# Where the last block's high parts are kept, and the order of the queue, at the start of the second SwiGLU product

## The chip, the cores and the metric

The kernel runs on one core of one Trainium2 chip. The metric is the device time of one execution in microseconds (us); the time of a kernel is the median of its runs. The engines are called as in the profile: PE (TensorE, matrix products), DVE (VectorE), ACT (ScalarE), POOL (GpSimd) and SP (SyncE, which here issues nearly all DMA transfers).

## The reference

One step of a decoder trunk with two layers, for a prompt of 1024 positions and 8 samples of 4 positions that share the weights. Layer 0 mixes tokens with windowed attention, layer 1 with a recurrent block. After each mixer comes a SwiGLU, and this is the part that the change concerns:

```python
def swiglu(h, w_in, w_out):
    g, u = jnp.split(h @ w_in, 2, axis=-1)
    return (jax.nn.silu(g) * u) @ w_out

# in every layer
xp = xp + yp
xs = xs + ys
xp = xp + swiglu(rms_norm(xp, ffn_norm[layer]), w_ffn_in[layer], w_ffn_out[layer])
xs = xs + swiglu(rms_norm(xs, ffn_norm[layer]), w_ffn_in[layer], w_ffn_out[layer])
```

The model width is 1024, the inner width 2816 (22 blocks of 128), all in 32-bit floats. One more output of layer 0 matters here: the new caches of the samples, most of which is a plain copy of the old ones.

## The kernel before, in words

**Tiles.** Columns are positions: 1056 of them in three column tiles, t = 0 and 1 of 384 and t = 2 of 288 (the end of the prompt and the samples). A product in 32-bit precision is made of three matrix products of rounded parts: `mm3` takes the high and the low part of the weights and of the data. A high part is a rounded copy made by ACT, the low part is the difference, made by DVE.

**First product.** `ffn_phase` goes through the 22 inner blocks. The first two are done plainly (`ins`); the other twenty by `blocks(f)`: `seven` treats t = 0 and 1 together as a 2 x 2 block scheme with seven products in place of eight, and `h_in` treats t = 2. The result of a block does not stay on the core: `keep` makes the high and the low part and stores both to `od` in device memory. Its source for the high part is one buffer of tag `hi` or, every second time, one of two buffers of tag `xs`. A pair of blocks gives seven such results for t = 0 and 1: the even block stores one of them, `keep_pair` of the odd block the other six. `h_in` stores one of its own.

**Second product.** `second` builds 20 units, five chunks of four blocks, with four units `mp` to a chunk. A unit gives two of the eight row blocks of the output. It has 66 matrix products: six for each of seven block products, and two times twelve of `plain` for t = 2. Its operands are the nine tiles of its chunk, in the order b11, t3, b21, t2, two for t = 2, t4, t1, b22, which `fetch(c, i, j)` loads from `od`. `add` adds each partial result onto the residual stream x on DVE (line 1026); these adds keep the order in which they are written. PE then goes on to accumulate in the same bank, so it waits for the add. The residual stream was put aside in device memory (`xd`) and comes back by `reload(0)` (row blocks 0 to 3, used by a chunk's units 0 and 1) and `reload(1)` (row blocks 4 to 7, used by units 2 and 3).

**Weights of a unit.** `Mixed` has three steps: `load` (line 151, DMA into one of two buffers `raw`), `parts` (`fill`: ACT at line 136 and DVE at line 137; then four sums on POOL, lines 157 to 160, that turn `raw` into the mixed weights), and `sums` (`fill` again on the mixed weights). Unit u's first step inside, `s0`, comes behind its third block product: it fetches three operands of the next chunk, does the `sums` of unit u + 1 and the `load` of unit u + 3. Behind the fourth product come the `parts` of unit u + 2. From `pin(True)` on, these keep their place among the adds on DVE.

**Order.** PE and SP issue in the order in which the program is written. ACT, DVE and POOL are put in order by a scheduler when the program is built, and then work through their lists in that order. `lead` is the hand-written order of the transition: the steps between and behind the last two blocks (`y` and `z`). `lead[3]` is the `mid` of the last block's `seven`, that is, behind its matrix products and ahead of its `keep_pair`; `lead[4]` comes behind that, ahead of the last `h_in`. In the kernel before, `lead[3]` queues six operands and `reload(1)`; the twelve stores of `keep_pair` follow; unit 2's weights come behind them.

**Places.** Large tiles live in 18 slots, taken from the front of a list and given back at its end (`act_tile`, `freeall`). In layer 0, `caches(b)` queues two copies from device memory to device memory ahead of each of the units 0 to 7.

Of the kernel before, what the change touches and what calls it, by code (L numbers as in the profile page):

```python
# [6 lines left out]
F32 = mybir.dt.float32  # L7
# [5 lines left out]
P = 128  # L13
# [9 lines left out]
DB, DS = 8, 4  # L23
# [12 lines left out]
WMAX = 384  # L36
# [129 lines left out]
class Whole:  # L166
# [5 lines left out]
    load = Mixed.load  # L172
# [81 lines left out]
class Kern:  # L254
# [589 lines left out]
    def ffn_phase(self, l, before, after):  # L844
# [7 lines left out]
        T, HD_, OD = {}, {}, {}  # L852
# [36 lines left out]
        def keep(dst, src):  # L889
            W = src.shape[-1]  # L890
            T["n"] = T.get("n", 0) + 1
            hi = self.tmp([P, WMAX], "hi", bufs=1) if T["n"] % 2 else \
                self.gt.tile([P, WMAX], F32, name=self.nm("hi"), tag="xs", bufs=2)
            hi = hi[:, :W]
            nc.scalar.activation(hi.bitcast(F32R), src, AF.Copy)  # L895
            tt(src.bitcast(F32R), src, hi, OP.subtract)
            nc.sync.dma_start(dst[:, 0, :], hi)
            nc.sync.dma_start(dst[:, 1, :], src)

        def keep_pair(f, h0, h1):  # L900

            c, j, half = place(f)
            g = lambda tag: self.gt.tile([P, WMAX], F32, name=self.nm("t"), tag=tag, bufs=2)
            od = lambda i: OD[c, i][:, j]
            if half == 0:
                st1 = T["even"] = (g("acc"), h1)
                tt(st1[0], h1, h0, OP.subtract)
                keep(od("b11"), h0)
                return
            t1, b12 = T.pop("even")  # L910
            t2, t4 = g("rs"), g("acc")
            tt(t2, h1, t1, OP.subtract)
            tt(b12, h1, b12, OP.subtract)
            tt(t4, h0, t2, OP.subtract)
            for i, x in zip(KEEP[1:], (h0, h1, t1, t2, b12, t4)):
                keep(od(i), x)


        def h_in(wg, wu, f, t, mid=(), last=False):
            W = WID[t]  # L920
            g = self.proj(wg, self.xn[t], W)
            for fn in mid:
                fn()
            u = self.proj(wu, self.xn[t], W)
            if last:
                self.freeall(self.xn[t])

            def post():
                sg = self.tmp([P, WMAX], "sg")
                nc.scalar.activation(sg[:, :W], g[:, :W], AF.Silu)  # L930
                tt(sg[:, :W], u[:, :W], sg[:, :W], OP.mult)
                c, j, half = place(f)
                keep((OD[c, j] if f >= NPL else HD_[t])[:, half], sg[:, :W])

            return post
# [32 lines left out]
        def unring():  # L968
            self.ring = []
            self.freeall(T["ring"])  # L970

        def reload(i):
            for t in range(NT):
                if i == 0:
                    self.xt[t] = []
                self.xt[t].append(self.act_tile([P, 4, WMAX], F32, "x"))
                nc.sync.dma_start(self.xt[t][i][0][:, :, :WID[t]], self.xd[t][:, 4 * i:4 * i + 4, :])
# [50 lines left out]
        def h_out(w0, w1, h, t, steps):  # L1028
            W = WID[t]
            ws = (w0, w1)  # L1030
            for m in range(KB):
                ps = self.bank()
                for c in range(2):
                    self.mm3(ps[:, :W], ws[c][:, 0, m * P:(m + 1) * P], ws[c][:, 1, m * P:(m + 1) * P],
                             h[:, c, 0, :W], h[:, c, 1, :W], c == 0, c == 1)
                x = self.xview(t, m)
                with tc.high_priority(PRI):
                    tt(x, ps[:, :W], x, OP.add)  # L1038
                if l == 1 or t < 2:
                    with tc.high_priority(PRI if t == 2 else 0):  # L1040
                        self.square(t, m, SQUARES[l][t][m])
                for fn in steps.get(m, ()):
                    fn()
# [12 lines left out]
        def unit(w, ws, o, mp, steps):  # L1056


            b11, t3, b21, t2, h0, h1, t4, t1, b22 = o
            m0, m1 = 2 * mp, 2 * mp + 1  # L1060

            def prod(ps, w, q, x, first):
                for j in range(2):
                    c = slice(q * 256 + j * P, q * 256 + (j + 1) * P)
                    self.mm3(ps[:, :WMAX], w[:, 0, c], w[:, 1, c], x[:, j, 0, :], x[:, j, 1, :],
                             first and j == 0, j == 1, not first)

            A, B, Dk = self.bank(), self.bank(), self.bank()
            prod(A, w, 0, b11, True)
            add(0, m0, A)  # L1070
            prod(Dk, ws, 2, t3, True)
            add(1, m1, Dk)
            prod(B, w, 1, b21, True)
            add(0, m0, B)
            steps[0]()
            prod(A, ws, 0, t2, False)
            add(0, m1, A)
            steps[1]()
            plain(w, (h0, h1), m0)
            prod(Dk, w, 3, t4, False)  # L1080
            add(0, m1, Dk)
            prod(A, ws, 3, t1, False)
            add(1, m1, A)
            plain(w, (h0, h1), m1)
            prod(A, ws, 1, b22, False)
            add(1, m0, A)
# [4 lines left out]
        def ins(f, mid=((), (), ())):  # L1091
            w = pair(f)
            return [Item(lambda a, b, t=t: h_in(a, b, f, t, mid[t]), w, w if t == 2 else []) for t in range(NT)]
# [7 lines left out]
        def second():  # L1101

            O = [[Operand(lambda c=c, i=i: OD[c, i], WMAX if isinstance(i, str) else WID[2], pools)
                  for i in ("b11", "t3", "b21", "t2", 0, 1, "t4", "t1", "b22")] for c in range(NCH)]
            M = [Mixed(I[f"wz{l}"][c, mp]) for c in range(NCH) for mp in range(4)]
            n = len(M)
            M += [Whole(I[f"wd{l}"][k]) for k in range(2)]
            H = [Operand(lambda t=t: HD_[t], WID[t], pools) for t in range(NT)]
            gate = Gate()

            def do(u, what):
                if u < len(M):
                    getattr(M[u], what)(self)

            def fetch(c, i, j):
                for o in O[c][i:j]:
                    assert o.prep(self)

            def pin(on):
                self.pinned = on  # L1120

            lead = [[lambda: reload(0), lambda: fetch(0, 0, 3)], [lambda: do(0, "load")],
                    [lambda: do(0, "parts"), lambda: do(0, "sums"), lambda: do(1, "load")],
                    [lambda: fetch(0, 3, 9), lambda: reload(1)], [lambda: do(1, "parts"), lambda: do(2, "load")],
                    [lambda: pin(True)], [lambda: pin(False), ring]]
            items = []
            for u in range(n):
                c, mp = divmod(u, 4)

                def s0(u=u, c=c, mp=mp):  # L1130
                    if mp < 3 and c + 1 < NCH:
                        fetch(c + 1, 3 * mp, 3 * mp + 3)
                    if mp < 3 and c + 1 == NCH:
                        assert H[mp].prep(self)
                    do(u + 1, "sums")
                    do(u + 3, "load")
                    gate.open = u == n - 1

                st = (s0, lambda u=u: do(u + 2, "parts"))
                p = [M[u].w, M[u].s]  # L1140
                items.append(Item(lambda a, b, *y, mp=mp, st=st: unit(a, b, y, mp, st), p + O[c],
                                  p + (O[c] if mp == 3 else []), [gate]))
            w = [x.w for x in M[n:]]
            steps = [{}, {2: n0[1:2], 5: n0[3:4]}, {2: n1[1:2], 5: n1[3:4]} if l else {3: n1[1:2], 6: n1[3:4]}]
            last = [Item(lambda a, b, h, t=t: h_out(a, b, h, t, steps[t]), w + [H[t]],
                         (w if t == 2 else []) + [H[t]], [gate]) for t in range(NT)]
            return lead, items, last

        L = [enter]
        a = ins(0, (before[1], (), ()))  # L1150
        b = ins(1, (before[3], (), ()))
        s = [lambda j=j: sums(j) for j in range(4)]
        L += before[0] + [a[0]] + before[2] + [b[0]] + before[4] + s[:2] + [a[1]] + s[2:] + [b[1]]
        L += [lambda: self.freeall(self.xn[1][:2]), a[2], b[2]]
        lead, units, p = second()
        for f in range(NPL, NF - 2):
            L += blocks(f)
# [1 line left out]
        z[0].mid = lead[3]  # L1159
        L += lead[0] + [y[0]] + lead[1] + [y[1]] + lead[2] + [z[0]] + lead[4] + [z[1]] + lead[5]  # L1160
        for i, x in enumerate(units):
            if l == 0 and i < DB:
                L.append(lambda b=i: self.caches(b))
            L.append(x)
        L += lead[6] + p[:2] + n0[4:] + [p[2]] + n1[4:]
        if l == 0:
# [377 lines left out]
```

## Time and profile before

| | us |
|---|---|
| median of 3 runs | 2177.17 |
| lowest and highest | 2175.77, 2177.6 |
| the profiled execution's own time | 2174.34 |
| its span in the profile | 2171.3 |
| PE busy in the span | 2117.0 |
| PE's mean granted clock | 0.991 |

The profiled execution is 2.8 us under the median, and its time lies 3.0 us above its span. Times in the views are microseconds from the start of the span. The second product of layer 0 begins at about 847.7, that of layer 1 at about 1907.7. In a time line each row is a start, a duration, an engine, a line of the kernel, an operation, output and inputs by the program's names, and a count; brackets give the idle time of the engine before it and what ended it. Names: `o` operands, `od` the stored results, `x` the residual stream, `xd` the stream put aside, `raw` weights as loaded, `w` their parts, `mm` a bank of results.

### The profile page before, as it was taken

To read this page: it belongs to the slowest core of one execution; us is meant where nothing else is said; L and a number is where in the kernel's file an instruction comes from. 1 tells how busy PE (TensorE), PEld (TensorE's weight loads), DVE (VectorE), ACT (ScalarE), POOL (GpSimd) and SP (SyncE) were. 2 spreads that over 40 slices of the span, in tenths; PEclk is the share of its full clock that TensorE was granted. 3 is DMA by queue.
4 is the path that set the end of the run, shared out by engine and by line. 5 is a ranking of instruction groups with operands and counts; after the bars stand their busy time and mean duration, and the time that the engine had idled before them with its cause. 6 is when DMAs were issued, how large, how long until landed. Compare 5 with 4: busy or idle time off the path is not lost.

```text
span 2171.3 us, 35218 instructions
## 1 busy us (share of the span) xinstructions
PE 2117.0 (97%) x13608; PEld 2093.8 (96%) x13608; DVE 1480.6 (68%) x2889; ACT 1005.4 (46%) x1835; POOL 253.4 (12%) x342
## 2 busy tenths in 40 slices
PE   9999999999999998999999989999999999989997
PEld 9899989999999998999999989999999999989997
DVE  6877787756656665666686787787666656556666
ACT  5666665434444343121268887754444444421112
POOL 1223231000000001322200000000000000022223
PEclk9999999999999999999999999999999999999999
DMA  5332335233343248755211123442343343585532
GB/s 194 100 102 85 116 125 179 100 105 130 116 154 133 101 153 328 283 215 187 94 49 59 59 82 113 148 154 78 126 144 133 105 158 120 219 318 216 209 141 80
DMA packets 131631, 310.10 MB, mean 143 GB/s; under 512 B 14152, under 2 KB 84872, under 8 KB 131464
## 3 DMA queue, kind: packets, MB, share of 16 engines
q1 hardware_dynamic: 130128, 306.95, 40.8%
q8 instruction: 106, 1.74, 0.3%
q10 hardware_dynamic: 1336, 0.92, 0.1%
q14 instruction: 61, 0.50, 0.1%
HBM read 223.15 MB, written 86.65 MB: 143 GB/s over the span
## 4 chain that ended last, share of the span: by engine, by line
PE 85%; DVE 6%; ACT 4%; DMA 3%; issue 1%; POOL 1%; SPq 0%; DVEq 0%; ACTq 0%; POOLq 0%
PE mm L314 81%; DMA o<-od 1%; ACT w L85 1%; DVE w L89 1%; PE pt L635 1%; PE s L587 1%; DVE s L605 1%; ACT s L612 1%; DMA od<-hi 1%; DMA raw<-in_wz 0%; DVE xn L353 0%; ACT g L1262 0%; PE mm L383 0%; DVE g L1310 0%; DVE pr L353 0%
## 5 line engine op out<-in xcount | busy, mean ns | idle before, releaser
L314 PE MATMUL mm<-xn,w 128*128 128x384 f32 (+1 forms) x5808 | 928.7, 318 | 12.3 <-DVE w L89 5.2
L314 PEld LDWEIGHTS mm<-xn,w 128*128 128x128 f32 x5808 | 903.2, 188 | 18.0 <-DVE w L89 6.3
L314 PE MATMUL mm<-o,w 128*128 128x384 f32 (+1 forms) x2928 | 474.0, 323 | 19.7 <-DVE x L1026 19.7
L314 PEld LDWEIGHTS mm<-o,w 128*128 128x128 f32 x2928 | 470.6, 189 | 20.8 <-DVE x L1026 20.8
L314 PE MATMUL mm<-T,w 128*128 128x384 f32 x1920 | 347.1, 336 | 0.1
L314 PEld LDWEIGHTS mm<-T,w 128*128 128x128 f32 x1920 | 334.8, 188 | 0.5 <-ACT e L999 0.4
L89 DVE TENSOR_TENSOR w<-raw,w 128x1024 fp32r<-128x1024 f32 x202 | 245.8, 1224 | 115.1 <-ACT w L85 113.6
L1026 DVE TENSOR_TENSOR x<-mm,x 128x384 f32<-128x384 f32 x360 | 191.2, 534 | 139.9 <-PE mm L314 139.0
L85 ACT ACTIVATE w<-raw 128x1024 fp32r<-128x1024 f32 x204 | 214.9, 1056 | 126.8 <-PE mm L314 65.9
L136 ACT ACTIVATE w<-raw 128x1024 fp32r<-128x1024 f32 x84 | 85.3, 1053 | 327.2 <-POOL raw L160 295.5
L157 POOL TENSOR_TENSOR raw<-raw 128x256 f32<-128x256 f32 x40 | 29.5, 738 | 1188.2 <-DVE w L137 1188.2
L137 DVE TENSOR_TENSOR w<-raw,w 128x1024 fp32r<-128x1024 f32 x84 | 102.8, 1224 | 15.4 <-ACT w L136 15.4
L627 POOL TENSOR_SCALAR s<-s,sm 128x256 f32<-128x256 f32 (+1 forms) x128 | 84.5, 679 | 203.9 <-DVE sm L625 84.3
L314 PE MATMUL mm<-att,w 128*128 128x384 f32 (+1 forms) x576 | 97.3, 325 | 0.0
L314 PEld LDWEIGHTS mm<-att,w 128*128 128x128 f32 x576 | 91.4, 188 | 1.9
L314 PE MATMUL mm<-y,w 128*128 128x384 f32 (+1 forms) x576 | 93.1, 322 | 0.0
L314 PEld LDWEIGHTS mm<-y,w 128*128 128x128 f32 x576 | 91.9, 188 | 0.0
L895 ACT ACTIVATE hi<-e 128x384 fp32r<-128x384 f32 x80 | 41.8, 523 | 87.4 <-DVE e L1017 33.1
L612 ACT ACTIVATE s<-s,sm 128x256 f32<-128x256 f32 (+1 forms) x128 | 61.7, 483 | 41.9 <-DVE sm L609 41.8
L118 DVE TENSOR_TENSOR w<-raw,w 128x1024 fp32r<-128x1024 f32 x40 | 48.9, 1222 | 35.9 <-ACT w L116 35.8
L374 ACT ACTIVATE sq<-x 128x384 f32<-128x384 f32 (+1 forms) x105 | 51.0, 492 | 38.2 <-DVE x L1038 18.0
L1001 DVE TENSOR_TENSOR sg<-mm,sg 128x384 f32<-128x384 f32 x40 | 22.2, 555 | 61.4 <-PE mm L314 61.4
(204 smaller groups left out, 2266.1 us busy)
## 6 DMA issues: line engine op xcount, KB each, us to landing
o<-od SPq DMA_DIRECT2D x70, 768.0 KB, 6.8
od<-hi SPq DMA_DIRECT2D x140, 192.0 KB, 2.0
raw<-in_wg SPq DMA_DIRECT2D x44, 512.0 KB, 4.1
raw<-in_wu SPq DMA_DIRECT2D x44, 512.0 KB, 4.5
raw<-in_wz SPq DMA_DIRECT2D x40, 512.0 KB, 3.7
od<-e SPq DMA_DIRECT2D x80, 192.0 KB, 2.0
raw<-in_wq SPq DMA_DIRECT2D x24, 512.0 KB, 3.6
raw<-in_wo SPq DMA_DIRECT2D x24, 512.0 KB, 3.6
```

What stands on the lines that cost most here:

```text
L85: nc.scalar.activation(self.t[:, 0, :], raw, AF.Copy)
L89: nc.vector.tensor_tensor(self.t[:, 1, :], raw, self.t[:, 0, :].bitcast(F32), OP.subtract)
L118: tt(d[:, 1, :], g, d[:, 0, :].bitcast(F32), OP.subtract)
L136: pin(nc.scalar.activation(self.t[:, 0, :], raw, AF.Copy))
L137: pin(nc.vector.tensor_tensor(self.t[:, 1, :], raw, self.t[:, 0, :].bitcast(F32), OP.subtract))
L157: tt(d, c, d, OP.add)
L314: mm = lambda *a, **k: self.nc.tensor.matmul(*a, skip_group_check=more, **k)
L374: nc.scalar.activation(sq[:, :W], self.xview(t, kb), AF.Square)
L612: nc.scalar.activation(s[:, j, :N], s[:, j, :N], AF.Exp, bias=sm[:, 1, j:j + 1], accum_out=sm[:, 3, j:j + 1])
L627: nc.gpsimd.tensor_scalar(s[:, j, :N], s[:, j, :N], sm[:, 4, j:j + 1], 1.0, op0=OP.mult, op1=OP.mult)
L895: nc.scalar.activation(hi.bitcast(F32R), src, AF.Copy)
L1026: tc.keep_in_program_order(tt(x, ps[:, :WID[t]], x, OP.add))
```

## The change

Three things change, in both layers where not said otherwise.

1. **Own places.** A new step `room` takes two slots, cuts them into eight places and gives the slots back to the list at once, so that whoever takes them next waits for what was done in them. While `T["room"]` exists, `keep` takes its places from it. It is made ahead of the last block's `keep_pair`, and `reload` removes it. The six high parts of that `keep_pair` go there.
2. **Order of the transition.** Behind the six operands, `lead[3]` now queues unit 2's weights instead of `reload(1)`. `reload(1)` moves behind the twelve stores, to the start of `lead[4]`. In unit 0, `s0` does the `sums` of unit 1 and the `load` of unit 3 ahead of the fetch of chunk 1's first three operands, no longer behind it.
3. **Cache copies** (layer 0 only). They stand ahead of the units 2 to 9 instead of 0 to 7.

No arithmetic is added or removed.

```diff
@@ keep
-            hi = self.tmp([P, WMAX], "hi", bufs=1) if T["n"] % 2 else \
-                self.gt.tile([P, WMAX], F32, name=self.nm("hi"), tag="xs", bufs=2)
+            if T.get("room"):
+                hi = T["room"].pop(0)
+            elif T["n"] % 2:
+                hi = self.tmp([P, WMAX], "hi", bufs=1)
+            else:
+                hi = self.gt.tile([P, WMAX], F32, name=self.nm("hi"), tag="xs", bufs=2)
@@ new, and reload
+        def room():
+
+            xs = [self.act_tile([P, 4, WMAX], F32, "hi") for _ in range(2)]
+            T["room"] = [x[0][:, k] for x in xs for k in range(4)]
+            self.freeall(xs)
+
         def reload(i):
+            T.pop("room", 0)
             for t in range(NT):
@@ second
-                    [lambda: fetch(0, 3, 9), lambda: reload(1)], [lambda: do(1, "parts"), lambda: do(2, "load")],
+                    [lambda: fetch(0, 3, 9), lambda: do(2, "load"), room],
+                    [lambda: reload(1), lambda: do(1, "parts")],
...
                 def s0(u=u, c=c, mp=mp):
+                    if u == 0:
+                        do(u + 1, "sums")
+                        do(u + 3, "load")
                     if mp < 3 and c + 1 < NCH:
                         fetch(c + 1, 3 * mp, 3 * mp + 3)
                     if mp < 3 and c + 1 == NCH:
                         assert H[mp].prep(self)
-                    do(u + 1, "sums")
-                    do(u + 3, "load")
+                    if u:
+                        do(u + 1, "sums")
+                        do(u + 3, "load")
@@ ffn_phase
-            if l == 0 and i < DB:
-                L.append(lambda b=i: self.caches(b))
+            if l == 0 and 2 <= i < DB + 2:
+                L.append(lambda b=i - 2: self.caches(b))
```

## The prediction

> **What bounds the kernel now.** I read the page's head first, then what the matmul engine waited for, then the stretch of the time line around its longest stop, once per layer.
>
> ```profile
> span 2171.3 us, 35218 instructions
> PE 2117.0 (97%) x13608; PEld 2093.8 (96%) x13608; DVE 1480.6 (68%) x2889; ACT 1005.4 (46%) x1835; POOL 253.4 (12%) x342
> PE mm L314 <- DVE x L1026: 19.7, 4, 8.9
> ```
>
> TensorE (PE) is the bound: 2117 of 2171 us. The largest item of its waiting is the accumulation `add` (L1026), 19.7 us in only four waits, the longest 8.9 us. The change touches just this place: two waits at the start of the second product in each layer. In the time line of layer 0 (start, duration, engine, line, operation; in brackets the idle time before it and what ended it):
>
> ```profile
> 836.35 4.21 SPq L204 DMA_DIRECT2D o<-od  x6
> 840.60 1.59 SPq L977 DMA_DIRECT2D x<-xd  x3
> 842.34 1.47 DVE L137 TENSOR_TENSOR w<-raw,w 128x1024 fp32r<-128x1024 f32 x1 [2.54 <-ACT w L136]
> 845.46 0.32 SPq L897 DMA_DIRECT2D od<-hi  x1
> 846.35 0.51 ACT L895 ACTIVATE hi<-t 128x384 fp32r<-128x384 f32 x1
> 847.75 3.34 PE L314 MATMUL mm<-o,w 128*128 128x384 f32 x18
> 848.28 0.55 DVE L896 TENSOR_TENSOR t<-t,hi 128x384 fp32r<-128x384 f32 x1
> 856.59 0.52 ACT L895 ACTIVATE hi<-e 128x384 fp32r<-128x384 f32 x1 [9.43 <-DMA od<-hi]
> 859.39 1.48 DVE L1026 TENSOR_TENSOR x<-mm,x 128x384 f32<-128x384 f32 x3
> 859.99 8.24 PE L314 MATMUL mm<-o,w 128*128 128x384 f32 x42 [8.90 <-DVE x L1026]
> 861.25 1.22 DVE L137 TENSOR_TENSOR w<-raw,w 128x1024 fp32r<-128x1024 f32 x1
> 861.77 0.38 SPq L151 DMA_DIRECT2D raw<-in_wz  x1
> 866.17 1.06 ACT L136 ACTIVATE w<-raw 128x1024 fp32r<-128x1024 f32 x1 [5.60 <-DMA raw<-in_wz]
> 869.84 10.38 PE L314 MATMUL mm<-o,w 128*128 128x384 f32 x63 [1.61 <-DVE x L1026]
> ...
> 1907.68 3.34 PE L314 MATMUL mm<-o,w 128*128 128x384 f32 x18
> 1919.75 9.06 PE L314 MATMUL mm<-o,w 128*128 128x384 f32 x42 [8.73 <-DVE x L1026]
> 1929.24 6.05 PE L314 MATMUL mm<-o,w 128*128 128x384 f32 x34 [0.42 <-DVE x L1026]
> ```
>
> At 836 SP queues six operands, at 840.6 the second halves of x, and only then come the stores of the last block's high parts. `keep` copies each high part into one of three buffers; after three copies (the third at 846.35) ACT must wait until a store has read its buffer, and that store lies behind everything queued earlier. So ACT's fourth copy comes at 856.59, DVE, which works through its list in order, sits at the subtraction behind it, and the first three adds come at 859.39. PE had done 18 matmuls of unit 0 by 851.1 and resumes at 859.99. A second, smaller stop follows: unit 2's weights, queued at 861.77, hold up ACT, then DVE, and PE until 869.84.
>
> **What the two stops cost.** Two more rows of DVE give a unit without a stop, one of PE the stretch behind:
>
> ```profile
> 885.33 1.22 DVE L137 TENSOR_TENSOR w<-raw,w 128x1024 fp32r<-128x1024 f32 x1
> 895.84 1.22 DVE L137 TENSOR_TENSOR w<-raw,w 128x1024 fp32r<-128x1024 f32 x1
> 869.84 75.33 PE L314 MATMUL mm<-o,w 128*128 128x384 f32 x471 [1.61 <-DVE x L1026]
> ```
>
> The same split in two successive units is 10.5 us apart. Unit 0 has 66 matmuls; its last six (1.1 us, a third of the 18 in 3.34) should start 10.5 - 1.1 = 9.4 us after the unit. They start at 869.84 against 847.75 + 9.4 = 857.15: 12.7 us lost. In layer 1: 1929.24 against 1917.08, 12.2 us. The waits are 8.90 + 1.61 and 8.73 + 0.42; the rest is 42 matmuls that took 8.24 and 9.06 where 9.4 - 3.3 = 6.1 is usual. The stretches (busy PE, weight load, DVE, ACT, POOL, then the granted clock, the DMA engines' share, GB/s) show why:
>
> ```profile
> 850.00:852.00 2.00, 1.10 (x7) 0.77 (x5) 0.00 (x0) 0.00 (x0) 0.00 (x0) 1.00 1.00 418
> 852.00:854.00 2.00, 0.00 (x0) 0.00 (x0) 0.00 (x0) 0.00 (x0) 0.00 (x0) 0.87 0.99 360
> 854.00:856.00 2.00, 0.00 (x0) 0.00 (x0) 0.00 (x0) 0.00 (x0) 0.00 (x0) 0.50 1.07 392
> 872.00:874.00 2.00, 2.00 (x14) 2.00 (x13) 1.11 (x2) 0.83 (x1) 0.00 (x0) 1.00 1.01 418
> 894.00:896.00 2.00, 2.00 (x13) 2.00 (x12) 1.19 (x3) 0.00 (x0) 0.00 (x0) 1.00 0.00 0
> ```
>
> The clock falls to 0.50 some 2.4 us after PE went idle (a mean of 0.87 over 852 to 854 means about half a microsecond at 0.50) and is slow when PE resumes. Stops under about 2.4 us should cost no clock. So 24.9 us stand to be had.
>
> **The change part by part.** Own places: eight slices of two free tiles take the six high parts of the last block, no instruction more. ACT's copies then follow their sources: the fourth to sixth at about 847 to 848.5 instead of from 856.59. DVE ends its third subtraction at 848.8, has three more of 0.55 and two narrower operations of the sample block, at most 2.8 together, and so reaches the first add near 851.5; PE wants it at 851.1. I put this at 0.4 us; it needs no term of its own, since it only moves the units' due times below, and the stops there end when the weights land. The 8.9 us stop and the slow clock behind it go.
>
> What is late next is the queue, since PE now runs 12 us earlier against the same bytes. Sizes:
>
> ```profile
> o<-od SPq DMA_DIRECT2D x70, 768.0 KB, 6.8
> od<-hi SPq DMA_DIRECT2D x140, 192.0 KB, 2.0
> raw<-in_wz SPq DMA_DIRECT2D x40, 512.0 KB, 3.7
> x<-xd SPq DMA_DIRECT2D x8, 768.0 KB, 12.0
> o<-od SPq DMA_DIRECT2D x20, 576.0 KB, 7.3
> out_nkc<-in_ck SPq DMA_DIRECT2D x8, 124.0 KB, 5.7
> 839.82 11.00 DMA o<-od
> ```
>
> New order behind the six operands, whose last lands at 850.8 (the chain's row 839.82 + 11.00), in MB: unit 2's weights 0.52; twelve stores 2.36; second halves of x (768 + 768 + 576 KB) 2.16; two stores of the sample block 0.29; unit 3's weights 0.52; chunk 1's first three operands 2.36; its next three (768 + 2 x 576 KB) 1.97; unit 4's weights 0.52. Pace: loads alone show 418, stretches with stores and x 360 to 392. I take 400, between them as the bytes are mixed. Landings: unit 2's weights 852.1, unit 3's (after 5.85 MB) 865.4, unit 4's (after 10.70 MB) 877.6, unit 5's (3.1 MB later) 885.4.
>
> When must they be there? In today's unit 1, which starts at 869.84 + 1.1 = 870.9, the weights of unit 3 came at 876.34, and PE did not stop (its row runs on for 75 us):
>
> ```profile
> 876.34 1.06 ACT L136 ACTIVATE w<-raw 128x1024 fp32r<-128x1024 f32 x1 [3.51 <-DMA raw<-in_wz]
> 878.58 1.38 DVE L1026 TENSOR_TENSOR x<-mm,x 128x288 f32<-128x288 f32 x3
> ```
>
> The adds behind them ended at 879.96; the last six matmuls of that unit were due at 870.9 + 9.4 = 880.3. So weights may come up to 5.8 us after a unit's start. Unit 0 starts at 847.75: due 853.5, there at 852.1, on time. Unit 1 starts at 858.25: due 864.05, there at 865.4, a stop of 1.4. Unit 2 starts at 868.75 + 1.4: due 875.95, there at 877.6, a further 1.6 (3.0 in all). Unit 5's are due at 885.05 + 3.0 and are on time. Neither stop reaches 2.4 us, so the clock should hold. Layer 1 has the same rows 59.9 us off, and I take 3.0 there too.
>
> Costed at nothing: x's second halves land near 863, and unit 2's first add is due near 871 with the stop; units 0 and 1 hide it (without them DVE would stand before that add, PE behind it). Unit 2's weight load is now ahead of the stores and waits in SP for unit 0's buffer, free at 842.34 + 1.47 = 843.8, before the first store exists (845.46). Unit 3's load, now ahead of chunk 1's operands, waits for unit 1's sums (L137, today at 861.25 because they sit behind the blocked copies, then near 852); what is queued covers that until about 864. Chunk 1's fourth and fifth operands get the tiles lent to the high parts, so SP waits there for stores that land near 858: covered too. The cache copies move by two units; they are 0.25 MB a unit, and their new last ones (units 8 and 9) meet a queue that has idle stretches such as 894 to 896.
>
> Sum: layer 0 12.7 - 3.0 = 9.7, layer 1 12.2 - 3.0 = 9.2, together 18.9 us. The profiled run took 2174.34 (span 2171.3), so 2155.4 on that footing; the median of the runs shown is 2177.17, 2.8 higher, which gives 2158.
>
> **The rivals.** (1) Nothing is late: if the queue moved 430 or more and the slack is a little larger, the whole 24.9 goes and the time is 2152. For it: 418 in two stretches quoted. Against: at 418 unit 4's weights still come at 876.4, 1.8 late. (2) The queue holds the pace of 360, the row of 852 to 854: unit 4's weights come at 880.5, 5.9 late in two stops of 3.0, both over 2.4, and the last slow clock adds about 2.1, as in layer 0 today. 7.9 a layer stay, 9.1 are won: 2168. By the Trainium skill, page DMA: Bandwidth & Descriptors, section Where 436 GB/s comes from, the HBM side binds such transfers at about 358 GB/s for a core, which would be this case; the stretches at 418 here do not agree with it. (3) Slower: SP stands at unit 3's load, because unit 1's sums are late on DVE, with all operands and unit 4's weights behind it. Its price is microsecond for microsecond once the queued bytes run out near 864; it outweighs the 9.7 when those sums end later than about 874. The row of today (861.25, even with the blockage) speaks against. (4) It does not do what it says: were a tile guarded as a whole, each copy into a slice would wait for the store of the slice before it, and the stop would stay: 2177.
>
> ```profile
> 2165.63 1.70 DVE x L1401 x4
> out_y<-x SPq DMA_DIRECT2D x4, 144.0 KB, 1.8
> ```
>
> Against (4): at the kernel's end DVE writes four slices of one tile in 1.70 us, while the store of a single slice takes 1.8.
>
> **How the numbers follow.** My forecast (2154 to 2163) gets 0.57; rival 1 0.15; rival 2 0.17; rival 4 0.05; rival 3 0.05; the last 0.01 is other gains. A measurement tells about 0.2%, 4.4 us, from no change: faster 0.90, same 0.05, slower 0.05. The range takes in rivals 1 and 2: 2151 to 2168.
>
> **What the profile after would show.** No idle time at L895 that a store ended; ACT's six copies within 4 us; the first adds of unit 0 near 851. Unit 2's weights landing near 852. PE stops of 1 to 2 us in units 1 and 2 behind L1026, with the weight load (raw) at the head of the chain there, and a granted clock of 1.00 throughout. PE's wait for L1026 falls from 19.7 to about 6. Wrong if ACT still waits for stores, if SP stands at a load while the DMA share falls under 0.9 between 850 and 875, or if one stop is long enough to drop the clock.

## The result, and the profile after

| | before | after |
|---|---|---|
| median of 4 runs, us | 2177.22 | 2160.87 |
| lowest and highest | 2175.77, 2177.6 | 2159.37, 2161.27 |
| profiled execution's own time | 2174.34 | 2161.13 |
| its span | 2171.3 | 2159.3 |

The ratio of the times is 0.9928, with a 95% interval of 0.9916 to 0.9939: 16.4 us faster, where 19 were forecast (2158, range 2151 to 2168). The two profiled executions differ by only 13.2, because that of before was 2.9 below its median and that of after 0.3 above.

The page of after, and a row of what PE waited for (engine, line, releaser: us in total, times, longest). Lines have moved: `add` is now L1037, the copy of a high part L899, its subtraction L900, the two stores L901 and L902, `reload` L988.

```profile
span 2159.3 us, 35215 instructions
PE 2117.7 (98%) x13608; PEld 2092.4 (97%) x13608; DVE 1480.1 (69%) x2889; ACT 1004.8 (47%) x1835; POOL 251.8 (12%) x342
PE mm L314 <- DVE x L1037: 6.5, 5, 2.9
```

PE does the same work in 12 us less of span; its wait for the adds fell from 19.7 us in four stops to 6.5 in five. The time line of layer 0 after:

```profile
848.59 0.53 ACT L899 ACTIVATE hi<-t 128x384 fp32r<-128x384 f32 x1
849.06 0.53 ACT L899 ACTIVATE hi<-e 128x384 fp32r<-128x384 f32 x1
849.53 0.53 ACT L899 ACTIVATE hi<-t 128x384 fp32r<-128x384 f32 x1
849.84 3.34 PE L314 MATMUL mm<-o,w 128*128 128x384 f32 x18
852.72 0.44 ACT L899 ACTIVATE hi<-sg 128x288 fp32r<-128x288 f32 x1 [2.37 <-DVE sg L935]
853.57 1.48 DVE L1037 TENSOR_TENSOR x<-mm,x 128x384 f32<-128x384 f32 x3
854.18 17.02 PE L314 MATMUL mm<-o,w 128*128 128x384 f32 x108 [1.00 <-DVE x L1037]
868.34 1.06 ACT L136 ACTIVATE w<-raw 128x1024 fp32r<-128x1024 f32 x1 [6.20 <-DMA raw<-in_wz]
872.01 10.82 PE L314 MATMUL mm<-o,w 128*128 128x384 f32 x66 [0.81 <-DVE x L1037]
879.97 1.06 ACT L136 ACTIVATE w<-raw 128x1024 fp32r<-128x1024 f32 x1 [4.98 <-DMA raw<-in_wz]
883.64 61.63 PE L314 MATMUL mm<-o,w 128*128 128x384 f32 x384 [0.82 <-DVE x L1037]
899.06 1.22 DVE L137 TENSOR_TENSOR w<-raw,w 128x1024 fp32r<-128x1024 f32 x1
```

The last three of the six copies run one behind the other, 0.47 us apart; none waits for a store. PE stops three times: 1.00 in unit 0 (behind the last block's small result, whose copy at 852.72 DVE had to wait for), 0.81 in unit 1 and 0.82 in unit 2, each behind weights that ACT was waiting for (868.34, 879.97). Layer 1 is not the same:

```profile
1901.62 3.34 PE L314 MATMUL mm<-o,w 128*128 128x384 f32 x18
1905.96 17.05 PE L314 MATMUL mm<-o,w 128*128 128x384 f32 x108 [1.00 <-DVE x L1037]
1922.20 1.06 ACT L136 ACTIVATE w<-raw 128x1024 fp32r<-128x1024 f32 x1 [7.84 <-DMA raw<-in_wz]
1925.87 69.36 PE L314 MATMUL mm<-o,w 128*128 128x384 f32 x422 [2.86 <-DVE x L1037]
1953.40 1.22 DVE L137 TENSOR_TENSOR w<-raw,w 128x1024 fp32r<-128x1024 f32 x1
```

**One number for a transition.** Without stops, the first split (L137) done in unit 4 would start 45.9 us after unit 0's first matmul: four units of 10.5, and 3.9 into the unit (before, unit 2 started at 881.4 and its split at 885.33). What is above 45.9 I call the loss. Before it was 12.7 and 12.1. After it is 899.06 - 849.84 - 45.9 = 3.3 in layer 0 and 1953.40 - 1901.62 - 45.9 = 5.9 in layer 1: 24.8 in all became 9.2, which is 15.6 of the 16.4 us between the medians. The two profiled executions themselves differ by 13.2: in that of after, unit 0 of layer 0 began 2.1 us later (849.84 against 847.75), the granted clock having been 0.98 over 0 to 100 and over 300 to 400 us, where before it was 1.00. The experiments below are read by the loss.

| kernel | loss, layer 0 | layer 1 | sum | median, us |
|---|---|---|---|---|
| before | 12.7 | 12.1 | 24.8 | 2177.2 |
| the change | 3.3 | 5.9 | 9.2 | 2160.9 |
| the change again | 3.5 | 5.9 | 9.4 | 2160.5 |
| own places alone | 12.9 | 12.8 | 25.7 | 2175.4 |
| order alone | 7.2 | 8.6 | 15.8 | 2167.3 |
| unit 3's load behind | 9.9 | 11.4 | 21.3 | 2171.9 |
| caches early | 5.6 | 3.8 | 9.4 | 2160.7 |
| x late | 3.1 | 7.5 | 10.6 | 2162.5 |
| unit 4's load ahead | 2.7 | 2.6 | 5.3 | 2156.4 |
| x late and unit 4's load ahead | 1.2 | 2.2 | 3.4 | 2154.8 |
| paired stores | 2.9 | 3.0 | 5.9 | 2158.0 |
| split stores | 11.3 | 11.0 | 22.3 | 2172.8 |
| paired stores and both loads | 0.7 | 0.5 | 1.2 | 2149.9 |

Median less loss is 2149 to 2152 in every row, so the differences in time are made in the transition, to within 2 us. The loss is that of one profiled execution, the median that of several; differences of less than 2 us between rows say little. One execution of "own places alone" (9012.6 us) and one of "paired stores and both loads" (6972.25) lie far above all others; the ratios leave them out, and without them these two medians are 2175.35 and 2149.67.

### The profile page after: what moved, and what is told of

Same layout as the page of the kernel before. It is cut to its first block, busy times and chain, and to the rows that moved or that the text cites. A ratio compares the mean times of both kernels' runs of the same rounds, so it can differ in the third digit from the quotient of the medians.

```text
span 2159.3 us, 35215 instructions
## 1 busy us (share of the span) xinstructions
PE 2117.7 (98%) x13608; PEld 2092.4 (97%) x13608; DVE 1480.1 (69%) x2889; ACT 1004.8 (47%) x1835; POOL 251.8 (12%) x342
## 4 chain that ended last, share of the span: by engine, by line
PE 80%; DVE 9%; ACT 5%; DMA 3%; issue 2%; POOL 0%; SPq 0%; ACTq 0%; DVEq 0%; POOLq 0%
PE mm L314 77%; DVE w L89 1%; ACT w L85 1%; DMA raw<-in_wz 1%; DVE s L605 1%; ACT s L612 1%; PE pt L635 1%; PE s L587 1%; ACT g L1278 1%; DMA raw<-in_wu 0%; DVE pr L353 0%; DVE xn L353 0%; DVE g L1326 0%; DVE acc L376 0%; DMA od<-hi 0%
## 5 line engine op out<-in xcount | busy, mean ns | idle before, releaser
L314 PE MATMUL mm<-xn,w 128*128 128x384 f32 (+1 forms) x5808 | 931.1, 318 | 12.7 <-DVE w L89 5.2
L1037 DVE TENSOR_TENSOR x<-mm,x 128x384 f32<-128x384 f32 x360 | 190.8, 534 | 140.1 <-PE mm L314 138.8
L137 DVE TENSOR_TENSOR w<-raw,w 128x1024 fp32r<-128x1024 f32 x84 | 102.8, 1224 | 16.4 <-ACT w L136 16.4
L899 ACT ACTIVATE hi<-e 128x384 fp32r<-128x384 f32 x80 | 41.8, 523 | 68.8 <-DVE e L1028 35.8
L899 ACT ACTIVATE hi<-sg 128x288 fp32r<-128x288 f32 (+1 forms) x52 | 23.7, 456 | 88.9 <-DVE sg L935 64.9
```

Source lines behind the costliest of these rows:

```text
L137: pin(nc.vector.tensor_tensor(self.t[:, 1, :], raw, self.t[:, 0, :].bitcast(F32), OP.subtract))
L314: mm = lambda *a, **k: self.nc.tensor.matmul(*a, skip_group_check=more, **k)
L1037: tc.keep_in_program_order(tt(x, ps[:, :WID[t]], x, OP.add))
```

## The experiments

The theory: PE's stops in the first units end when the weights of a later unit have landed, and that is set by what is queued ahead of them; the buffers only come first in line. The rivals: the buffers made the stop and the order is a detail; or the limit is not bytes but how many transfers there are.

**Own places alone.** The queue keeps the order of before.

```diff
-                    [lambda: fetch(0, 3, 9), lambda: do(2, "load"), room],
-                    [lambda: reload(1), lambda: do(1, "parts")],
+                    [lambda: fetch(0, 3, 9), lambda: reload(1), room],
+                    [lambda: T.pop("room", 0), lambda: do(1, "parts"), lambda: do(2, "load")],
```

Here `reload` does not remove `T["room"]`; `s0` and the cache copies are as before.

> The last block's high parts get their own places, but the queue keeps the order of before (second halves of x, then the stores, then unit 2's weights; fetch ahead of unit 3's load; cache copies at units 0 to 7). Theory 1 (what PE waits for is the weights behind the queued bytes, the buffers only come first): the ACT wait for stores vanishes, but unit 2's weights still lie behind 4.33 + 2.16 + 2.36 MB and land about 863 against 866 before, so unit 0 stops at its last product for about 10 us and the clock falls; 10 to 12 us lost per layer where before lost 12.4, and a time of 2172 to 2177. Theory 2 (the three buffers made the stop, the order is a detail): the loss per layer is that of the whole change, 3 to 6 us, and the time 2160 to 2164.

2175.38 us, ratio to before 0.9997 (0.9987 to 1.0007): no change. ACT and PE in layer 0:

```profile
847.25 0.53 ACT L899 ACTIVATE hi<-e 128x384 fp32r<-128x384 f32 x1
864.18 1.06 ACT L136 ACTIVATE w<-raw 128x1024 fp32r<-128x1024 f32 x1 [11.89 <-DMA raw<-in_wz]
867.85 77.44 PE L314 MATMUL mm<-o,w 128*128 128x384 f32 x469 [8.91 <-DVE x L1036]
```

The wait for the stores is gone (the copy of `e` that came at 856.59 before comes at 847.25), and the stop is back whole, 42 matmuls later: 8.91 us behind unit 2's weights. Theory 2 of that run falls.

**Order alone.** No own places.

```diff
-                    [lambda: fetch(0, 3, 9), lambda: do(2, "load"), room],
+                    [lambda: fetch(0, 3, 9), lambda: do(2, "load")],
```

> The order of the queue as in the whole change, without the own places: the last block's high parts use the three buffers. Theory 1: ACT's fourth copy waits for the first store, which now lies behind 4.85 MB instead of 6.5 and lands 6 to 7 us after the first matmul of unit 0 instead of 11; PE stops 5 to 6 us there, the clock falls (another 1.5 to 2), and the later stops shrink because the queue catches up meanwhile: 6 to 9 us lost per layer, time 2164 to 2170. Theory 2: the stop of 8.9 us stays nearly whole, time 2172 to 2177.

2167.33 us, ratio 0.9960 (0.9945 to 0.9975). ACT's copy waits for the store as expected, and the stop is 4.88 us:

```profile
854.38 0.52 ACT L899 ACTIVATE hi<-e 128x384 fp32r<-128x384 f32 x1 [5.50 <-DMA od<-hi]
857.70 29.03 PE L314 MATMUL mm<-o,w 128*128 128x384 f32 x174 [4.88 <-DVE x L1037]
```

So the order alone takes 9 us off the loss, the places alone nothing, both together 15.6. The places pay only when the weights behind them are early.

**Unit 3's load behind.** In `s0` of unit 0 the fetch comes first again; all else is the change.

```diff
-                    if u == 0:
-                        do(u + 1, "sums")
-                        do(u + 3, "load")
                     if mp < 3 and c + 1 < NCH:
...
-                    if u:
-                        do(u + 1, "sums")
-                        do(u + 3, "load")
+                    do(u + 1, "sums")
+                    do(u + 3, "load")
```

> The whole change, but in unit 0 the fetch of chunk 1's first three operands stands ahead of unit 1's sums and unit 3's load, as before. Theory 1 (bytes ahead of the weights set the stops): 2.36 MB at 400 GB/s, 5.9 us later for unit 3's weights, a stop of 6 to 8 us in unit 1 and a fallen clock; 8 to 11 us lost per layer, time 2167 to 2172. Theory 2 (the later stops come from something else than the order of these loads): 2160 to 2163.

2171.92 us, ratio to before 0.9982 (0.9972 to 0.9992). One stop of 6.67 us in unit 1 of layer 0, 7.43 in layer 1:

```profile
878.50 66.83 PE L314 MATMUL mm<-o,w 128*128 128x384 f32 x406 [6.67 <-DVE x L1037]
```

This small swap is worth 11 of the 16 us: without it the stop moves from unit 0 to unit 1 and keeps most of its size.

**Caches early.** The cache copies ahead of units 0 to 7.

```diff
-            if l == 0 and 2 <= i < DB + 2:
-                L.append(lambda b=i - 2: self.caches(b))
+            if l == 0 and i < DB:
+                L.append(lambda b=i: self.caches(b))
```

> The whole change, but the cache copies stand ahead of units 0 to 7 as before (layer 0 only). Theory 1: 0.5 MB and four more transfers ahead of unit 4's weights, 1 to 2 us more stop in layer 0, none in layer 1, time 2161.5 to 2163.5. Theory 2 (too little to matter): 2161.

2160.71 us: no difference in the median. In layer 0 the loss was 5.6 where the two executions of the change show 3.3 and 3.5, as expected; but layer 1, whose program is the same, showed 3.8 instead of 5.9. The sum hides the effect, and the spread of the four runs is wider than it: two are near 2157, among them the profiled one, and two near 2164. Whether the moved copies help stays open.

**x late.** The second halves of x behind unit 3's weights.

```diff
-                    [lambda: reload(1), lambda: do(1, "parts")],
+                    [lambda: do(1, "parts")],
...
                     if u == 0:
                         do(u + 1, "sums")
                         do(u + 3, "load")
+                    if u == 0:
+                        reload(1)
```

> The whole change, with the second halves of x queued behind unit 3's weights (in unit 0) instead of ahead of them. Theory 1 (a unit's stop ends when the bytes ahead of its weights have moved): 2.16 MB less ahead of unit 3's weights, so the stop in unit 1 goes; the bytes ahead of unit 4's weights are the same, so the stop in unit 2 takes its place, and the loss stays at 3 to 6 us a layer: time 2159 to 2163. Theory 2 (the second halves are the load that hurts): 2155 to 2158.

2162.53 us, within its spread (2158.34 to 2163.82) the same as the change. The stop in unit 1 went, that in unit 2 grew: 1.67 us in layer 0, 3.78 in layer 1. Moving bytes from ahead of one load to ahead of the next moves the stop, as theory 1 has it.

**Unit 4's load ahead.** In `s0`, unit 1 does as unit 0.

```diff
-                    if u == 0:
+                    if u < 2:
                         do(u + 1, "sums")
...
-                    if u:
+                    if u >= 2:
                         do(u + 1, "sums")
```

> The whole change, and in unit 1, too, the sums of the next unit and unit 4's load stand ahead of the fetch. Theory 1: 1.97 MB less ahead of unit 4's weights (4.9 us), the stop in unit 2 goes, those of units 0 and 1 (1.0 and 0.8 us in layer 0) stay: 1.8 to 3 us lost per layer, time 2156 to 2159. Theory 2 (SP now stands at this load until unit 2's sums are done, and the queue runs dry behind it): no gain, 2160 to 2164.

2156.41 us, ratio 0.9910 (0.9895 to 0.9924). The stop in unit 2 is gone in both layers; those in units 0 and 1 stay (0.99 and 1.32 in layer 0). SP's stand at this load did no harm.

**Both.** The last two edits together.

> Both moves: the second halves of x behind unit 3's weights, and unit 4's weights ahead of the fetch in unit 1. Theory 1: all weights of units 2 to 4 are in time, only DVE's backlog in unit 0 stays (1.0 us): 1 to 2 us lost per layer, time 2153 to 2157. Theory 2 (the queue as a whole is short, whatever the order): the stop moves on to unit 3 or to the second halves of x in unit 2, time 2158 to 2162.

2154.78 us, ratio 0.9900 (0.9886 to 0.9915). In layer 0 only unit 0's 0.99 us is left:

```profile
853.91 91.39 PE L314 MATMUL mm<-o,w 128*128 128x384 f32 x575 [0.99 <-DVE x L1037]
```

**Paired stores.** This one and the next ask what held layer 1. In the built program SP waits, ahead of every transfer, on one of eight counters taken in turn, for the transfer eight places before it (place in SP's list, line, output and input, what it waits for):

```
345 L151 DMA raw_9191<-in_wz 128x1024 [waits DMAHW3_49,DVE_49]
353 L902 DMA od_4790<-t_9199 128x384 [waits DMAHW3_49,DVE_49]
361 L901 DMA od_4794<-hi_9294 128x288 [waits DMAHW3_49,Activation_49]
```

The counter of a transfer is the one that it raises itself when it lands, and the eight come round in turn for the whole program. So at most eight are under way, and twelve stores of 192 KB fill that limit with few bytes. In layer 1 of the change SP's own waits and the stretches (clock, DMA share and GB/s at the end) show it:

```profile
SPq L901 <- DMA o<-od: 1.0, 1, 1.0
SPq L902 <- DMA raw<-in_wz: 0.8, 1, 0.8
...
1906.00:1908.00 2.00, 2.00 (x13) 2.00 (x14) 2.00 (x4) 0.32 (x1) 0.00 (x0) 1.00 0.98 366
1908.00:1910.00 2.00, 2.00 (x15) 2.00 (x14) 1.67 (x3) 0.74 (x1) 0.00 (x0) 1.00 0.49 184
1926.00:1928.00 2.00, 2.00 (x9) 2.00 (x10) 0.65 (x2) 0.22 (x1) 1.59 (x3) 0.67 1.01 423
1928.00:1930.00 2.00, 2.00 (x8) 2.00 (x7) 0.64 (x2) 0.84 (x1) 0.00 (x0) 0.50 1.04 378
```

SP stood at two stores until an operand and unit 2's weights had landed (1.8 us together); then it had only small stores to issue, and the queue ran half empty. The edit puts both parts of a result side by side and stores them with one transfer:

```diff
             if T.get("room"):
-                hi = T["room"].pop(0)
+                pl = T["room"].pop(0)[:, :, :W]
+                nc.scalar.activation(pl[:, 0, :].bitcast(F32R), src, AF.Copy)
+                tt(pl[:, 1, :].bitcast(F32R), src, pl[:, 0, :], OP.subtract)
+                nc.sync.dma_start(dst, pl)
+                return
...
-            xs = [self.act_tile([P, 4, WMAX], F32, "hi") for _ in range(2)]
-            T["room"] = [x[0][:, k] for x in xs for k in range(4)]
-            self.freeall(xs)
+            xs = T["places"] = [self.act_tile([P, 4, WMAX], F32, "hi") for _ in range(3)]
+            T["room"] = [x[0][:, 2 * k:2 * k + 2] for x in xs for k in range(2)]
...
-                    [lambda: pin(True)], [lambda: pin(False), ring]]
+                    [lambda: self.freeall(T.pop("places")), lambda: pin(True)], [lambda: pin(False), ring]]
```

> The whole change, with the high and the low part of each of the last block's six results side by side and stored by one DMA instead of two (three slots instead of two). The built program has SP wait, ahead of each transfer, for the one eight places before it, so at most eight are under way; in layer 1 SP stood among the small stores and the queue ran half empty from 1908 to 1910. Theory A (this limit costs layer 1 its longer stop): six transfers fewer, no dry stretch, 2.5 to 4 us lost in either layer, time 2157.5 to 2159.5. Theory B (only bytes count): no change, 2160 to 2162.

2157.99 us, ratio 0.9919 (0.9904 to 0.9934); 2.9 and 3.0 lost. The medians alone do not prove the gain: the four runs go from 2155.73 to 2161.68, the eight of the change (two rows of the table) from 2158.54 to 2163.75. Some 20 us from about the start of unit 0, first in the change, then in its second execution, then with pairs (two rows of each):

```profile
850.00:870.00 20.00, 19.00 (x119) 18.68 (x119) 13.61 (x24) 4.82 (x7) 2.94 (x4) 1.00 1.03 385
1902.00:1922.00 20.00, 19.00 (x119) 18.68 (x118) 12.83 (x23) 3.66 (x5) 2.95 (x4) 1.00 0.95 349
```

```profile
850.00:870.00 20.00, 19.01 (x119) 18.69 (x118) 13.43 (x25) 4.90 (x7) 2.94 (x4) 1.00 1.03 384
1902.00:1922.00 20.00, 19.00 (x120) 18.68 (x119) 12.61 (x23) 3.51 (x4) 2.94 (x4) 1.00 1.01 369
```

```profile
850.00:870.00 20.00, 19.64 (x123) 19.31 (x123) 13.38 (x25) 6.18 (x9) 2.95 (x4) 1.00 1.03 408
1902.00:1922.00 20.00, 19.64 (x124) 19.32 (x123) 13.69 (x25) 6.06 (x9) 2.97 (x4) 1.00 1.03 411
```

The pace rises from 385 and 349 (384 and 369) to 408 and 411, and the two layers become alike. Pairing also makes the rows longer, 3072 bytes in place of 1536. In the traces' packet records a row of 1536 bytes took 65 ns on its engine, one of 3072 took 121; for the 2.36 MB of stores on 16 engines that is about 0.5 us, an estimate from these records. It could explain what unit 3's weights gained in layer 0 (0.4 us), not the 2.5 us that they gained in layer 1.

**Split stores.** The other way: each store of the last block in two halves, the same bytes.

```diff
-            nc.sync.dma_start(dst[:, 0, :], hi)
-            nc.sync.dma_start(dst[:, 1, :], src)
+            for k, y in enumerate((hi, src)):
+                for h in range(2 if T.get("room") else 1):
+                    c = slice(h * W // 2, (h + 1) * W // 2) if T.get("room") else slice(0, W)
+                    nc.sync.dma_start(dst[:, k, c], y[:, c])
```

> The whole change, with each of the last block's twelve stores cut into two transfers of half the columns: the same bytes, twelve transfers more. Theory A (the number of transfers under way, or the time SP takes for each, bounds the pace among the stores): the queue runs half empty in both layers, unit 3's and 4's weights come 2 to 5 us later than in the whole change, 6 to 9 us lost per layer, time 2164 to 2169. Theory B (only bytes count): 2160 to 2162.

2172.77 us, 12 slower than the change, and a loss of 11.3 and 11.0, more than either theory gave. In layer 0 the queue runs half empty while SP issues two halves in about 0.85 us, and emptier where two took 2.72:

```profile
855.30 0.85 SPq L904 DMA_DIRECT2D od<-hi  x2
856.25 0.85 SPq L904 DMA_DIRECT2D od<-t  x2
858.17 2.72 SPq L904 DMA_DIRECT2D od<-e  x2
...
854.00:856.00 2.00, 2.00 (x16) 2.00 (x15) 2.00 (x4) 0.05 (x1) 0.00 (x0) 1.00 0.68 226
856.00:858.00 2.00, 2.00 (x14) 2.00 (x13) 1.70 (x3) 0.00 (x0) 1.07 (x2) 1.00 0.61 200
858.00:860.00 2.00, 2.00 (x16) 2.00 (x15) 0.80 (x2) 0.00 (x0) 1.84 (x3) 1.00 0.33 101
878.56 66.71 PE L314 MATMUL mm<-o,w 128*128 128x384 f32 x407 [8.37 <-DVE x L1039]
```

So bytes alone do not set the pace: the same bytes in twice as many transfers cost 12 us, and the pairs point the same way. Which limit it is, is not shown: two halves are 0.197 MB, so 0.85 us for the two is 231 GB/s by issue time alone, and the limit of eight acts beside it. The halves have shorter rows, too: 768 bytes took 36 ns where 1536 took 65, about 0.7 us for all the stores by the same estimate, far from 12.

**All together.** Paired stores, x late, unit 4's load ahead.

> All three together: paired stores, the second halves of x behind unit 3's weights, unit 4's weights ahead of the fetch in unit 1. Theory 1 (stops end when the bytes ahead of a unit's weights have moved, and eight transfers under way bound the pace): the weights are in time, DVE's backlog in unit 0 costs 0.4 as in the paired kernel, 0.5 to 2 us lost per layer, time 2152 to 2155. Theory 2 (the two cures mend the same stop, so they do not add): as with both loads ahead, 2154 to 2156.

2149.88 us, ratio 0.9876 (0.9859 to 0.9893), 11 us under the change and below the range forecast. 0.7 and 0.5 us are lost; one stop of 0.36 is left in either layer:

```profile
851.47 93.82 PE L314 MATMUL mm<-o,w 128*128 128x384 f32 x588 [0.36 <-DVE x L1040]
```

The cures nearly add: from the 9.2 of the change, pairs alone take 3.3 and the two moved loads 5.8; together they take 8.0.

**The change again.**

> The changed kernel itself once more, for the spread of its stops. If layer 1's longer stop (2.86 us) belongs to that layer's program, it comes again, 5.5 to 6.5 us lost in layer 1 and 3.4 in layer 0. If it is a matter of how a single execution's transfers land, layer 1 lies between 3.4 and 6, layer 0 likewise, the sum between 7 and 11.

2160.51 us, 3.5 and 5.9 lost, with a stop of 2.96 in layer 1 again. But up to unit 3's load layer 1 has the same program in "caches early" and in "unit 4's load ahead", too, and the stop in unit 1 was 1.35 and 1.17 there. So the long stop came in two executions of four: it is not fixed by that layer's program. Nor does it need the dry stretch: in this second execution SP did not stand at those two stores, and its lowest 2 us there still moved 287 GB/s. What goes with the stop is when SP gets to unit 3's load (L151). In us from unit 0's first matmul:

| kernel, layer | load issued | weights taken up by ACT | stop in unit 1 |
|---|---|---|---|
| paired stores, 0 | 8.1 | 18.1 | 1.01 |
| paired stores, 1 | 9.5 | 18.1 | 1.03 |
| the change, 0 | 9.9 | 18.5 | 0.81 |
| the change again, 0 | 10.2 | 18.7 | 0.98 |
| unit 4's load ahead, 1 | 10.4 | 18.9 | 1.17 |
| unit 4's load ahead, 0 | 10.6 | 19.0 | 1.32 |
| caches early, 1 | 10.6 | 19.1 | 1.35 |
| the change again, 1 | 11.5 | 20.7 | 2.96 |
| caches early, 0 | 11.6 | 20.3 | 2.56 |
| the change, 1 | 12.3 | 20.6 | 2.86 |
| split stores, 1 | 17.2 | 25.2 | 7.51 |
| split stores, 0 | 17.9 | 26.1 | 8.37 |

The weights come 8 to 10 us after the load is issued, and SP issues it when it is through with the stores and the second halves of x. In the second execution it lost its time at one store that took 1.82 us to issue, not some 0.4; the trace does not say why.

## Why the prediction was right, point by point

- **The two stops as the whole of what could be had:** right. 15.6 of the 16.4 us came from there, and the kernel with 1.2 us of loss left takes 2150.
- **Own places end the wait for stores:** right, but alone they gave nothing. The prediction said "What is late next is the queue" and costed the parts only together; the run with places alone shows how much hung on that sentence.
- **DVE's backlog:** forecast 0.4, measured a stop of 1.00 in either layer. DVE reached the first add when forecast, 3.7 us after the first matmul (853.57 - 849.84; forecast 851.5 - 847.75), by two slips that cancel: operations behind one another start 0.47 us apart where 0.55 was counted, and the sample block's subtraction waited 0.51 us for ACT's copy. Left out was the add itself: PE goes on 0.6 us after an add has begun (854.18 against 853.57; before, 859.99 against 859.39). With paired stores the first add began 3.1 us after the first matmul, and the stop was 0.36. That the backlog needs no term of its own held in layer 0, where the landing of the weights set the end; in "unit 4's load ahead" and "both" it is what remains.
- **Due times and landings in layer 0:** forecast, counted from the first matmul, unit 3's weights at 17.7 us and unit 4's at 29.9; ACT took them up at 868.34 - 849.84 = 18.5 and 30.1. Loss forecast 3.0, measured 3.3 and 3.5. The pace of 400 was near 385. The single stops were not those forecast, 1.00, 0.81 and 0.82 in units 0, 1 and 2 for 0, 1.4 and 1.6; the sum holds because the last landing sets it.
- **Layer 1, "I take 3.0 there too":** this is the term that was mis-sized, 5.9 measured. Unit 3's weights came at 20.6 us and not 17.7. The step that failed is the pace, "I take 400" from the bytes ahead: it has no term for when SP gets to a load, and SP is held up among the small stores, at most eight transfers being under way (unit 3's load issued 12.3 us after the first matmul, 9.9 in layer 0; 349 GB/s over 20 us, 184 at the worst). Why it was held up longer in layer 1 in two executions, and not in two others, stays open. The stop of 2.86 us then also cost clock, 0.67 and 0.50 in the quoted stretches, which the prediction had only in rival 2. Layer 1 was that rival in part.
- **Its signs of being wrong:** one came, in layer 1: a stop "long enough to drop the clock". No copy waited for a store, and between 850 and 875 the DMA share stayed at 0.94 or more in layer 0. The 2.4 us below which a stop "should cost no clock" came from one stop and is no rule (last section).
- **Rival 2 and the page:** the Trainium skill, page DMA: Bandwidth & Descriptors, section Where 436 GB/s comes from, has about 358 GB/s bind between HBM and the core's memory. Layer 1's 349 looks like it, but the paired stores moved the same bytes at 411 in the same place, so the measurement decides against it here.
- **Rival 1** would have needed 430; the best pace in this stretch was 411 to 415. Its time of 2152 was passed another way, by pairs and by late bytes behind the loads (2150). **Rival 3** (SP standing at unit 3's load for unit 1's sums) did not come; those sums ended at 856.2 in layer 0 and SP reached the load at 859.8. **Rival 4** fell with the copies 0.47 us apart into slices of the same tiles.
- **Sum:** 18.9 forecast, 15.6 found in the transition, 16.4 between the medians. Of the 3.3 us missing in the transition 2.9 are layer 1's.

## What to carry to other kernels

Where an engine waits for a buffer that a store must leave, look at what it would wait for next before giving it more buffers: here the buffers alone gave nothing, the order alone 9 us, both 16. Give each load a due time from the consumer's rows and count what lies ahead of it, in bytes and in transfers: with eight transfers under way, joining two small stores into one took 3.3 us off the loss, nearly as much as moving unit 4's load (3.9). When a stop moves instead of vanishing, put the late bytes behind the next load, too, until nothing is late.

## What the runs showed of the hardware that was not expected

A stop of 2.56 us is enough to halve the clock, and the fall may come after PE has resumed. In "caches early" PE stopped for 2.56 us, until 871.78:

```profile
870.00:872.00 2.00, 0.22 (x1) 0.22 (x2) 2.00 (x5) 0.00 (x0) 1.41 (x2) 1.00 1.02 426
872.00:874.00 2.00, 2.00 (x10) 2.00 (x10) 0.65 (x2) 0.30 (x1) 1.51 (x3) 0.77 1.00 411
874.00:876.00 2.00, 2.00 (x8) 2.00 (x8) 0.56 (x1) 0.76 (x1) 0.00 (x0) 0.50 1.06 384
```

The granted clock was 1.00 during the stop and 0.50 two microseconds after it. The Trainium skill, page TensorE: Matmul & The Clock Gate, section What's actually happening, has the clock fall after an idle window of about 3.4 us that runs freely; stops of 2.56, 2.86 and 2.96 us were enough here, one of 1.67 was not. The length of one stop does not decide. Before, stops of 1.61 and 2.31 us with two matmuls between them (1287.7 to 1292.1) brought the clock to 0.50; in the profiled execution of the change it was 0.50 over 316 to 318, with no stop over 0.8 us since 304, and before it stayed at 1.00 in that part of the program. In the clock records of all thirteen traces a spell at 0.50 inside a kernel lasted 3.41 us, or two or three times that.

One thing stays open: SP took 5.11 us, not some 0.35, to issue unit 4's weights in layer 0 of the change (867.57 to 872.68), and 4.96 in layer 1. The split whose buffer the load needs had ended at 866.64, and the trace does not say what SP stood at. The DMA engines moved 421 GB/s or more meanwhile, so nothing shows that it cost time.
